# The thirty-third feature's Fourier weights: from own products to the sine product's free rows

## The chip, the core and the metric

The kernel runs on one core of one Trainium2 chip. A core has five engines that run at the same time, each through its own list of instructions and in the order of that list: TensorE (PE; its weight loads are shown as PEld), VectorE (DVE), ScalarE (ACT), GpSimd (POOL) and SyncE (SP), which here only issues transfers (its queue is shown as SPq). Products land in PSUM, a small memory of banks of 128 partitions x 512 f32; DVE and ACT read them from there ("evacuate" them) and so give the bank back to PE. Transfers between the chip's memory and SBUF, or within SBUF, run on 16 DMA engines. Engines wait for each other by semaphores only.

The metric is the device time of one execution in microseconds. It is measured in several runs. A further execution is profiled; the profile's span goes from its first instruction to its last.

## The reference, cut to what matters

Two inputs, a prompt of 256 positions and a sample of 2048, go through one encoder layer each, with the same weights. All is f32.

```python
F_GROUPS = 8; F_GROUP_DIM = 64; F_WIDTH = 512

def fourier_mix(u, w_f, b_f):
    b, s, _ = u.shape
    ug = u.astype(jnp.float32).reshape(b, s, F_GROUPS, F_GROUP_DIM)
    spec = jnp.fft.fft2(ug, axes=(1, 3), norm='ortho')
    mixed = spec.real.reshape(b, s, F_WIDTH).astype(u.dtype)
    return mixed @ w_f + b_f

def encoder_layer(x, ...):
    h = rms_norm(x, g_pre)
    q, k, v, z_a, u_f, z_f = jnp.split(h @ w_in, ...)
    y_a = neighbourhood_attention(q, k, v, rpb)
    y_f = fourier_mix(u_f, w_fourier, b_fourier)
    mixed = concatenate([rms_norm(y_a, g_na) * silu(z_a), rms_norm(y_f, g_f) * silu(z_f)])
    return x + rms_norm(mixed @ w_out, g_post)
```

The change lies in fourier_mix: a two-dimensional transform, over the positions and over the 64 features of each of eight groups, of which the real part is kept, and a product with the weights `w_fourier` (512 x 512).

## The kernel before, in words

**Stages.** The kernel computes the projections (q, k, v, z_a, z_f and u) for the sample first, with the transform over the positions half done; then comes the Fourier stage, 549 to 607 us, which the change touches; then the attention over 36 groups, and the output product. An f32 product with full precision is three passes here: both operands are split into a rounded "high" part (ACT copies it into the type fp32r) and a rest ("low", DVE subtracts), and `mm3` (L164 to L166) does high x high, high x low, low x high. So most products are followed by an ACT copy and a DVE subtraction: `split_ps` (L1016, L1017).

**The mathematics of the stage.** The real part of the transform over a group's 64 features is a cosine product minus a sine product. Feature s and feature 64 - s have the same cosines and opposite sines, so they are folded: 32 slots, s = 0 to 31, do for each of the two, plus the thirty-third, s = 32, whose cosine at frequency f is (-1)^f and whose sine is zero. Instead of transforming the data over the features, the kernel transforms the weights: `pq(0)` multiplies `w_fourier` with the cosines, `pq(1)` with the sines. The slot 0 of the sines is free, since sin 0 = 0: the table `cs` holds zeros there. The thirty-third feature's weights, `w32` (96 partitions x 512: eight groups at every fourth partition of three blocks of 32, the middle block for the low part), are made by products of their own in `pq32`, from a table `c32` of (-1)^f.

**Order of the stage on PE**, written by hand in the code: four groups `gq` 0 to 3, each of five column chunks c in `stage2` (tile `pab`; L1024 are the small products of `dft`, four of them for each chunk). Group 0 also makes `pny`, group 2 also the prompt's part `pup` (from `up` and `f256`). Results are split into AB (tiles `abh`, `abl`) and, for the chunk c = 4, into `a32`. Behind group 2 comes `pq(0)`, behind group 3 come `pq(1)` (L1062) and `pq32` (L1069). Then come the output products `y_mm` (tile `py`): for each block e of 128 output features (0 to 3) and each third ti of the columns, in the order 2, 0, 1, twelve products into p1 and p2 and one with `w32` and `a32`. `y_out` evacuates: ACT adds the bias (t1), DVE combines t1 and p2 into `Y` (L1276), a tile of 128 x 2304 f32 (1.2 MB) with two buffers. Y's prompt part is stored by L1302, the rest, 1 MB, by L1325, and `y0` is loaded from the stored prompt part (L1321) and from zD (L1322). ACT and POOL also make squares of Y for the norm.

**PSUM.** Eight banks: tag "a" has three (ppq, pny, pup, py1), "b" two (two thirds of the pab, and py2), "c" one (the other third of pab), "t" two.

**Buffers and transfers.** In this stretch the Tile scheduler orders the lists of ACT, DVE, POOL and SP; it does so ahead of time, and on the chip the order is fixed. All loads and stores here are issued by SP. In its order before: `f256` (L996), `up` (L998), the four loads of the last z tiles (L831), `cs` (L1001), `c32` (L1003, 192 KB), `wf` (L1005, 1 MB, the weights); then for the attention: the keys' rows `kl` (L1091, two halves), the tables `tb` (L1105, L1106, L1109), the queries `ql` (L1135), `v` (L1152, L1154), `za` (L1159), the output weights `wo` (L1234, eight loads), and the stores and loads of Y. A transfer takes one of eight completion semaphores in turn, and its issue waits until the transfer that is eight ahead in the list has landed; it also waits until its tile is free, or its data are there.

Of the kernel before, what the change touches and what calls it, by code (L numbers as in the profile page):

```python
# [10 lines left out]
F32 = mybir.dt.float32  # L11
F32R = mybir.dt.float32r
AF = mybir.ActivationFunctionType
ALU = mybir.AluOpType
# [29 lines left out]
def constants():  # L44
    c = {}
    c["ident"] = np.eye(128, dtype=np.float32)
    n1 = np.arange(128)
    f1 = np.zeros((128, 128))
    for k1 in range(64):
        f1[:, 2 * k1] = np.cos(2 * np.pi * ((k1 * n1) % 128) / 128)  # L50
        f1[:, 2 * k1 + 1] = np.sin(2 * np.pi * ((k1 * n1) % 128) / 128) if k1 else (-1.0) ** n1
    c["f1"] = f1.reshape(32, 4, 128).transpose(1, 0, 2).reshape(128, 128)
    nrm = 1.0 / np.sqrt(2048 * 64)
    n2 = np.arange(16)
    d = np.zeros((128, 16, 128))
    for g in range(16):
        for kl in range(4):
            k1 = 4 * g + kl
            for k2 in range(16):
                if k1:  # L60
                    k = k1 + 128 * k2
                elif k2 < 8:
                    k = 128 * k2
                else:
                    k = 64 + 128 * (k2 - 8)
                co = np.cos(2 * np.pi * ((n2 * k) % 2048) / 2048) * nrm
                si = np.sin(2 * np.pi * ((n2 * k) % 2048) / 2048) * nrm
                ca = k2 * 4 + kl
                cb = 64 + ca
                r0 = (kl * 2) * 16 + n2  # L70
                r1 = (kl * 2 + 1) * 16 + n2
                if k1:
                    d[r0, g, ca] = co
                    d[r1, g, ca] = -si
                    d[r0, g, cb] = si
                    d[r1, g, cb] = co
                else:
                    r = r0 if k2 < 8 else r1
                    d[r, g, ca] = co
                    d[r, g, cb] = si  # L80
    c["d2"] = d
    dn = np.zeros((128, 2))
    dn[:16, 0] = ((-1.0) ** n2) * nrm
    c["dnyq"] = dn
    n = np.arange(256)[:, None]
    k = np.arange(129)[None, :]
    ang = 2 * np.pi * ((n * k) % 256) / 256
    f256 = np.concatenate([np.cos(ang), np.sin(ang)], axis=1) / np.sqrt(256 * 64)
    c["f256"] = f256.reshape(4, 2, 32, 258).transpose(0, 2, 1, 3).reshape(128, 2, 258)
    f = np.arange(64)  # L90
    sl = np.arange(32)
    cs = np.zeros((128, 2, 64))
    c32 = np.zeros((128, 4, 96))
    for b in range(2):
        rows, cols = slice(64 * b, 64 * b + 64), slice(32 * b, 32 * b + 32)
        ang = 2 * np.pi * ((f[:, None] * sl[None, :]) % 64) / 64
        cs[rows, 0, cols] = np.cos(ang)
        cs[rows, 1, cols] = np.where(sl == 0, 0.0, np.sin(ang))
        for x in range(4):
            for r in range(3):  # L100
                c32[rows, x, 32 * r + 4 * (2 * x + b)] = (-1.0) ** f
    c["cs"] = cs
    c["c32"] = c32
    cm = np.zeros((128, 2, 40))
    cs_ = np.zeros((128, 80))
    rm = np.zeros((128, 48))
    for p in range(128):
        for b in range(2):
            ws = min(max(32 * b + p % 32 - 8, 0), 48)
            kc = 24 * b + np.arange(40)  # L110
            cm[p, b] = np.where((kc >= ws) & (kc < ws + 16), 0.0, BIG)
        i, qc = divmod(p, 16)
        for cb, j in ((0, slice(0, 24)), (1, slice(24, 56)), (3, slice(56, 80))):
            ws = min(max(16 * cb + qc - 8, 0), 48)
            kc = KC0[cb] + np.arange(KW[cb])
            cs_[p, j] = np.where((kc >= ws) & (kc < ws + 16), 0.0, BIG)
        for r0, j in ((max(i - 4, 0), np.arange(11)), (i, 11 + np.arange(15)), (min(i, 4), 26 + np.arange(12))):
            rm[p, j] = np.where((j - j[0] >= r0) & (j - j[0] < r0 + 8), 0.0, BIG)
    c["cmask"] = cm.reshape(128, 80)
    c["csmask"] = cs_  # L120
    c["rmask"] = rm
    return {k: np.ascontiguousarray(v.astype(np.float32)) for k, v in c.items()}
# [40 lines left out]
def mm3(nc, out, lh, ll, rh, rl, first, last):  # L163
    nc.tensor.matmul(out, lh, rh, start=first, stop=False)  # L164
    nc.tensor.matmul(out, lh, rl, start=False, stop=False)  # L165
    nc.tensor.matmul(out, ll, rh, start=False, stop=last)  # L166


def build(tc, A, O):
    nc = tc.nc  # L170
    es = ExitStack()
    es.enter_context(tc.manual_schedule(engines={mybir.EngineType.PE}))
    cst = es.enter_context(tc.tile_pool(name="cst", bufs=1))
# [28 lines left out]
    invt = cst.tile([128, 18], F32, name="invt")  # L202
    invf = cst.tile([128, 18], F32, name="invf")
    inva = cst.tile([128, 18], F32, name="inva")
    dnyq = cst.tile([128, 2], F32, name="dnyq")
    cm = cst.tile([128, 2, 40], F32, name="cm")


# [5 lines left out]
    ps = es.enter_context(tc.tile_pool(name="ps", bufs=3, space=PSUM))  # L214
    mmc = [0]

    def mmt(n):
        x = mmc[0] % 5 > 2
        mmc[0] += 1
        return ps.tile([128, n], F32, tag="t" if x else "a", name="mm", bufs=2 if x else 3)  # L220
# [10 lines left out]
    def gt(shape, dtype, name):  # L231
        return gp.tile(shape, dtype, tag="g", name=name)
# [152 lines left out]
    nq = {}  # L385
# [332 lines left out]
    for c in range(3, 6):  # L718
# [7 lines left out]
        if c == 4:  # L726
# [33 lines left out]
    for b in range(16):  # L760
# [13 lines left out]
        if 2 <= b < 8:  # L774
            x, y = divmod(b, 2)
# [7 lines left out]
        p = mmt(512)[:, :TP]  # L783
# [55 lines left out]
    for i in range(16):  # L839
# [48 lines left out]
        for j in range(7):  # L888
# [29 lines left out]
            if sg == 0:  # L918
                x, y = divmod(7 * (pr - 1) + j, 14)
# [17 lines left out]
            for f, d in ((u_load, 0), (u_split, 4), (u_stage1, 6)):  # L937
                x = 7 * pr + j - 7 - d
# [11 lines left out]
            p = mmt(512)  # L950
# [41 lines left out]
        nc.vector.memset(x, 0.0)  # L992
    pg = ExitStack()
    sm = pg.enter_context(tc.tile_pool(name="smF", bufs=1))
    f256 = sm.tile([128, 2, 258], F32, name="f256")
    nc.sync.dma_start(f256, A["f256"])  # L996
    up = sm.tile([128, 2, 512], F32, name="up")
    nc.sync.dma_start(up, uD.rearrange("(t p) c -> p t c", p=128))  # L998
    zgs.append(load_z(3))
    cs2 = sm.tile([128, 2, 64], F32, name="cs2")  # L1000
    nc.sync.dma_start(cs2, A["cs"])  # L1001
    c32 = sm.tile([128, 4, 96], F32, name="c32")
    nc.sync.dma_start(c32, A["c32"])  # L1003
    wf = sm.tile([128, 4, 512], F32, name="wf")
    nc.sync.dma_start(wf, A["wf"])  # L1005

# [8 lines left out]
    def split_ps(dh, dl, src, vec=False):  # L1015
        nc.vector.tensor_copy(dh, src) if vec else nc.scalar.copy(dh, src)  # L1016
        nc.vector.tensor_tensor(out=dl, in0=src, in1=dh.bitcast(F32), op=ALU.subtract)  # L1017
# [32 lines left out]
            dft(p, c, [(up[:, t], f256[:, t, 129 * m:129 * m + 129]) for t in range(2)])  # L1050
            split_ab(gq, c, lambda a: a[:, 1025:1154], p)

    PQ = []
    w32 = ab.tile([96, 512], F32R, name="w32")

    def pq(m):
        h = gt([128, 2, 512], F32R, "pqh")
        l = gt([128, 2, 512], F32R, "pql")
        for c in range(2):
            p = ps.tile([128, 512], F32, tag="a", name="ppq")  # L1060
            for x in range(2):
                nc.tensor.matmul(p[64 * x:64 * x + 64], cs2[:, m, :], wf[:, 2 * c + x, :], start=True, stop=True)  # L1062
            split_ps(h[:, c], l[:, c], p)
        PQ.append((h, l))

    def pq32():
        p = ps.tile([96, 512], F32, tag="a", name="ppq")
        for c in range(4):
            nc.tensor.matmul(p, c32[:, c], wf[:, c], start=c == 0, stop=c == 3)  # L1069
        nc.scalar.copy(w32, p)  # L1070
        nc.vector.tensor_tensor(out=w32[32:64], in0=p[32:64], in1=w32[32:64].bitcast(F32), op=ALU.subtract)

    for gq in range(4):
        for c in range(5):
            stage2(gq, zgs[gq], c)
        if gq == 2:
            pq(0)
    pq(1)
    pq32()
    pg.close()  # L1080

    KQ = T // 4
# [158 lines left out]
    sm = pg.enter_context(tc.tile_pool(name="smY", bufs=2))  # L1241
# [10 lines left out]
    def y_mm(e, ti):  # L1252
# [5 lines left out]
        for m, p in ((0, p1), (1, p2)):  # L1258
            for c in range(2):
                mm3(nc, p[:, :n], PQ[m][0][:, c, es_], PQ[m][1][:, c, es_],  # L1260
                    AB[m][0][:, c, cs], AB[m][1][:, c, cs], c == 0, m == 1 and c == 1)
# [109 lines left out]
    sm = pt.enter_context(tc.tile_pool(name="smA", bufs=2))  # L1371
# [202 lines left out]
    for k in range(2, len(G) + 1):  # L1574
        pr, i = divmod(k, 9)
        g, f = G[k] if k < len(G) else None, G[k - 1] if k else None
# [19 lines left out]
        x = k // 2 + 1  # L1596
# [62 lines left out]
        if 32 <= k < 36:  # L1659
            x, d = k - 32, atiles[k - 32]  # L1660
# [122 lines left out]
```

## Time and profile before

| | us |
|---|---|
| runs, without a profile | 970.62, 971.44, 972.39 |
| their median | 971.44 |
| the profiled execution, its span | 968.7 |
| of it, PE busy | 958.9 |

The clock granted to TensorE was 0.998 of full speed over the span. The page lists for each engine how long it was busy. The chain of waits is found from the end: from the last instruction back to what released it, or to the one before it on its engine, and so on. Rows of a timeline read "start, duration, engine, line, operation, output tile <- input tiles, shape", with the idle time ahead of it and what ended that in brackets; "x8" is a run of eight instructions, and then the duration is that of the whole run. Rows of a list of waits read "engine, line <- who released it: total, count, largest". A transfer's landing isn't in the timeline of its queue, whose rows are issues: it is read from the instruction that waits for it.

### The profile page before, as it was taken

What the parts mean: (1) busy time and instruction counts of PE and PEld (TensorE: products, weight loads), DVE (VectorE), ACT (ScalarE), POOL (GpSimd) and SP (SyncE); (2) the same over time, 40 slices, a digit from 0 to 9 for tenths busy, and PEclk for the clock granted to TensorE, in tenths of its full rate; (3) what the DMA queues carried; (4) which work ended last, traced back from release to release, by engine and by line L of the source; (5) the groups of instructions that cost most, each with busy time, mean ns of one, the idle gap of its engine ahead of it and who ended that gap; (6) DMA issues with size and microseconds to landing.
All of it is one profiled execution on the core that took longest, in us unless ns stands there. A gap on an engine that the chain in (4) does not pass through costs nothing.

```text
span 968.7 us, 17031 instructions
## 1 busy us (share of the span) xinstructions
PE 958.9 (99%) x5769; PEld 801.0 (83%) x5769; DVE 709.5 (73%) x1306; ACT 497.5 (51%) x1078; POOL 430.2 (44%) x400
## 2 busy tenths in 40 slices
PE   9999999999999999999999999999999999999997
PEld 7889988888888888888888879887788888878886
DVE  6768987777986867787777446776665656649997
ACT  6836675433325533333344255677666776744443
POOL 3100003464752202756654033577677686624544
PEclk9999999999999999999999999999999999999999
DMA  9899696556849996599989898698887998979993
GB/s 327 312 373 357 234 366 240 194 189 252 318 163 377 352 410 239 211 371 320 322 303 339 301 328 300 210 281 273 258 240 234 286 327 270 296 244 331 330 346 129
DMA packets 146450, 279.89 MB, mean 289 GB/s; under 512 B 13162, under 2 KB 84284, under 8 KB 142972
## 3 DMA queue, kind: packets, MB, share of 16 engines
q1 hardware_dynamic: 145932, 278.41, 82.4%
q8 instruction: 46, 0.75, 0.3%
q10 hardware_dynamic: 432, 0.39, 0.1%
q14 instruction: 40, 0.33, 0.1%
HBM read 184.37 MB, written 101.72 MB: 295 GB/s over the span
## 4 chain that ended last, share of the span: by engine, by line
PE 96%; DVE 1%; ACT 1%; issue 1%; POOL 1%; DMA 0%; DVEq 0%; SPq 0%; POOLq 0%; ACTq 0%
PE po L1432 19%; PE mm L165 18%; PE mm L164 18%; PE mm L166 18%; PE pv L1521 5%; PE ptb L1505 5%; PE s L1181 4%; PE pab L1024 2%; PE py L164 1%; PE py L166 1%; PE py L165 1%; DMA gpre<-gpre 0%; PE ppq L1062 0%; PE pz L166 0%; PE pz L164 0%
## 5 line engine op out<-in xcount | busy, mean ns | idle before, releaser
L164 PE MATMUL mm<-xh,wa 128*128 128x512 f32 x448 | 174.4, 389 | 0.0
L165 PE MATMUL mm<-xl,wa 128*128 128x512 f32 x448 | 174.3, 389 | 0.0
L166 PE MATMUL mm<-xh,wa 128*128 128x512 f32 x448 | 174.3, 389 | 0.0
L536 POOL TENSOR_TENSOR ws<-wr 128x512 f32<-128x512 f32 x16 | 22.2, 1386 | 226.6 <-DMA wr<-wz 222.8
L1215 POOL TENSOR_SCALAR w<-w,m 128x480 f32<-128x480 f32 (+6 forms) x136 | 86.0, 644 | 46.3 <-DVE m L1212 35.9
L164 PEld LDWEIGHTS mm<-xh,wa 128*128 128x128 f32 x448 | 84.1, 188 | 17.6
L166 PEld LDWEIGHTS mm<-xh,wa 128*128 128x128 f32 x448 | 84.1, 188 | 17.5
L165 PEld LDWEIGHTS mm<-xl,wa 128*128 128x128 f32 x448 | 84.1, 188 | 17.4
L1432 PE MATMUL po<-wo,yh 128*128 128x512 f32 x272 | 90.4, 413 | 0.0
L551 DVE TENSOR_TENSOR wa<-wr,wa 128x512 fp32r<-128x512 f32 x60 | 68.5, 1149 | 27.1 <-ACT wa L550 26.8
L1208 ACT ACTIVATE w<-w,m 128x480 f32<-128x480 f32 (+6 forms) x136 | 79.3, 586 | 17.1 <-DVE m L1203 17.1
L1432 PE MATMUL po<-w,yh 128*128 128x512 f32 x280 | 86.7, 391 | 0.0
L1203 DVE CUSTOM_DVE_ANT_1 w<-s,tb 128x360 f32<-128x360 f32 (+5 forms) x124 | 62.4, 541 | 10.3 <-PE s L1181 9.8
L589 POOL TENSOR_TENSOR mt<-mt,rmask 128x880 f32<-128x880 f32 (+2 forms) x24 | 51.0, 2139 | 34.1 <-DVE mt L585 27.6
L165 PE MATMUL mm<-vl,xh 128*128 128x512 f32 x168 | 65.5, 390 | 0.2 <-DVE vl L482 0.2
L164 PE MATMUL mm<-vh,xh 128*128 128x512 f32 x168 | 65.4, 389 | 0.0
L166 PE MATMUL mm<-vh,xl 128*128 128x512 f32 x168 | 65.4, 389 | 0.0
L877 DVE TENSOR_TENSOR f<-u,mm 128x512 f32<-128x512 f32 x64 | 43.5, 680 | 28.0 <-PE mm L166 23.1
L1432 PEld LDWEIGHTS po<-w,yh 128*128 128x128 f32 x280 | 52.3, 188 | 10.9 <-issue 0.2
L1505 PE MATMUL ptb<-ident,w 128*120 128x128 f32 (+5 forms) x428 | 59.5, 276 | 1.0 <-ACT nsb L1481 0.9
L550 ACT CAST wa<-wr 128x512 fp32r<-128x512 f32 x60 | 36.4, 617 | 44.1 <-PE mm L166 23.2
L1521 PEld LDWEIGHTS pv<-pt,v 120*64 120x64 f32 (+6 forms) x896 | 48.2, 136 | 12.8 <-issue 9.6
(263 smaller groups left out, 2394.3 us busy)
## 6 DMA issues: line engine op xcount, KB each, us to landing
wr<-wz SPq DMA_DIRECT2D x48, 512.0 KB
vl<-sD SPq DMA_DIRECT2D x20, 512.0 KB
xm<-xm SPq DMA_DIRECT2D x9, 1024.0 KB
oD<-ofs SPq DMA_DIRECT2D x18, 512.0 KB
of<-oD SPq DMA_DIRECT2D x18, 512.0 KB
yr<-yD SPq DMA_DIRECT2D x34, 256.0 KB
zD<-f SPq DMA_DIRECT2D x16, 512.0 KB
woD<-wo SPq DMA_DIRECT2D x16, 512.0 KB
```

The costliest lines, as they stand in the source:

```text
L164: nc.tensor.matmul(out, lh, rh, start=first, stop=False)
L165: nc.tensor.matmul(out, lh, rl, start=False, stop=False)
L166: nc.tensor.matmul(out, ll, rh, start=False, stop=last)
L551: nc.vector.tensor_tensor(out=o[:, 1], in0=src, in1=o[:, 0].bitcast(F32), op=ALU.subtract)
L589: nc.gpsimd.tensor_tensor(out=o, in0=i, in1=rmask[:, m0:m0 + n].unsqueeze(2).to_broadcast([128, n, 80]), op=ALU.add)
L877: nc.vector.tensor_tensor(out=dst(f, b), in0=src(uu[u]), in1=src(p), op=op)
L1203: nc.vector.tensor_tensor_reduce(out=rows(g["w"][b][:, h, :n], w), in0=rows(g["s"][2 * b + h][:, :n], w), in1=tv, scale=1.0, scalar=3.0e38 ...
L1208: nc.scalar.activation(w, w, AF.Exp, bias=m[:, h:h + 1], scale=-1.0, accum_out=m[:, 2 + h:3 + h])
L1215: nc.gpsimd.tensor_scalar(w, w, m[:, 4 + h:5 + h], 1.0, ALU.mult, ALU.mult)
L1432: nc.tensor.matmul(p, (d["l"] if x == 2 else d["h"])[:, c], w(n, int(x == 1), c), start=j == 0, stop=j == 11)
L1505: nc.tensor.transpose(ptb[h][:nk, j * 128:j * 128 + 128], g["w"][b][:, h, c0:c0 + nk], ident)
L1521: nc.tensor.matmul(p[hs, b], g["v"][:nk, v, hs], g["pt"][b][:nk, h, j * 128:j * 128 + 128], start=j == 0, stop=j == len(ch) - 1)
```

## The change

The sine table gets (-1)^f in its free slot 0, so that `pq(1)` makes the thirty-third feature's weights along with the sines' (partitions 0, 32, 64 and 96 of its two result tiles), and `pq32` with its table `c32` goes. For this,

- `pq(1)` moves from behind group 3 to between groups 1 and 2, and the loads of `cs` and `wf` move ahead of those of `f256`, `up` and the last z tiles;
- in `pq(1)`, DVE copies each result tile to an SBUF tile `nq` (two buffers), and for each of the two tiles three transfers of 4 x 512 f32 (8 KB) bring the four rows to their places in `nw` (96 x 512, filled with zeros by POOL before). They are issued by SP;
- the split of the sine product masks the free slot away with a third column of `dnyq` (0 at each 32nd partition, else 1): ACT's copy has it as a scale, and DVE's subtraction becomes a scalar_tensor_tensor, product x mask - high;
- `w32` is made from `nw` as it was from the product before, a copy by ACT and a subtraction by DVE.

```diff
-    dn = np.zeros((128, 2))
+    dn = np.zeros((128, 3))
     dn[:16, 0] = ((-1.0) ** n2) * nrm
+    dn[:, 2] = np.arange(128) % 32 != 0
...
-    c32 = np.zeros((128, 4, 96))
...
-        cs[rows, 1, cols] = np.where(sl == 0, 0.0, np.sin(ang))
-        for x in range(4):
-            for r in range(3):
-                c32[rows, x, 32 * r + 4 * (2 * x + b)] = (-1.0) ** f
+        cs[rows, 1, cols] = np.where(sl == 0, (-1.0) ** f[:, None], np.sin(ang))
...
+    cs2 = sm.tile([128, 2, 64], F32, name="cs2")
+    nc.sync.dma_start(cs2, A["cs"])
+    wf = sm.tile([128, 4, 512], F32, name="wf")
+    nc.sync.dma_start(wf, A["wf"])
+    nw = sm.tile([96, 512], F32, name="nw")
+    nc.gpsimd.memset(nw, 0.0)
     f256 = sm.tile([128, 2, 258], F32, name="f256")
     nc.sync.dma_start(f256, A["f256"])
     up = sm.tile([128, 2, 512], F32, name="up")
     nc.sync.dma_start(up, uD.rearrange("(t p) c -> p t c", p=128))
     zgs.append(load_z(3))
-    cs2 = sm.tile([128, 2, 64], F32, name="cs2")
-    nc.sync.dma_start(cs2, A["cs"])
-    c32 = sm.tile([128, 4, 96], F32, name="c32")
-    nc.sync.dma_start(c32, A["c32"])
-    wf = sm.tile([128, 4, 512], F32, name="wf")
-    nc.sync.dma_start(wf, A["wf"])
...
     def pq(m):
...
-            split_ps(h[:, c], l[:, c], p)
-        PQ.append((h, l))
-
-    def pq32():
-        p = ps.tile([96, 512], F32, tag="a", name="ppq")
-        for c in range(4):
-            nc.tensor.matmul(p, c32[:, c], wf[:, c], start=c == 0, stop=c == 3)
-        nc.scalar.copy(w32, p)
-        nc.vector.tensor_tensor(out=w32[32:64], in0=p[32:64], in1=w32[32:64].bitcast(F32), op=ALU.subtract)
+            if m == 0:
+                split_ps(h[:, c], l[:, c], p)
+                continue
+            nq_ = sm.tile([128, 512], F32, name="nq", bufs=2)
+            nc.vector.tensor_copy(nq_, p)
+            for r in range(3):
+                nc.sync.dma_start(nw[32 * r + 16 * c:32 * r + 16 * c + 16:4], nq_[::32])
+            nc.scalar.activation(h[:, c], p, AF.Copy, scale=dnyq[:, 2:3])
+            nc.vector.scalar_tensor_tensor(out=l[:, c], in0=p, scalar=dnyq[:, 2:3], in1=h[:, c].bitcast(F32),
+                                           op0=ALU.mult, op1=ALU.subtract)
+        PQ[m] = h, l
+        if m:
+            nc.scalar.copy(w32, nw)
+            nc.vector.tensor_tensor(out=w32[32:64], in0=nw[32:64], in1=w32[32:64].bitcast(F32), op=ALU.subtract)
 
     for gq in range(4):
         for c in range(5):
             stage2(gq, zgs[gq], c)
-        if gq == 2:
-            pq(0)
-    pq(1)
-    pq32()
+        if gq in (1, 2):
+            pq(2 - gq)
     pg.close()
```

By the order in which the scheduler puts the changed kernel's instructions on their engines, SP issues the six `nw` transfers behind the last z tiles' loads and ahead of `kl`; from there on the order of its transfers is that of before. ACT has, behind `pq(0)`'s first copy, the copy of `nw` to `w32`, and the copies of `kl` among those of group 3.

More of the change, by code (lines that the diff above doesn't have):

```diff
@@ L97, in constants @@
         cs[rows, 0, cols] = np.cos(ang)
-        cs[rows, 1, cols] = np.where(sl == 0, 0.0, np.sin(ang))
-        for x in range(4):
-            for r in range(3):
-                c32[rows, x, 32 * r + 4 * (2 * x + b)] = (-1.0) ** f
+        cs[rows, 1, cols] = np.where(sl == 0, (-1.0) ** f[:, None], np.sin(ang))
     c["cs"] = cs
-    c["c32"] = c32
     cm = np.zeros((128, 2, 40))
@@ L204, in build @@
     inva = cst.tile([128, 18], F32, name="inva")
-    dnyq = cst.tile([128, 2], F32, name="dnyq")
+    dnyq = cst.tile([128, 3], F32, name="dnyq")
     cm = cst.tile([128, 2, 40], F32, name="cm")
@@ L1051, in stage2 @@
             split_ab(gq, c, lambda a: a[:, 1025:1154], p)
-    PQ = []
+    PQ = {}
     w32 = ab.tile([96, 512], F32R, name="w32")
```

## The prediction

> **What bounds the kernel now.** I read the page first, then the waits, then the stretch that the change touches: the Fourier stage, 549 to 607 us. From the page, busy time and the chain by engine; from the list of waits, all of PE's from 545 us to the end:
>
> ```profile
> PE 958.9 (99%) x5769; PEld 801.0 (83%) x5769; DVE 709.5 (73%) x1306; ACT 497.5 (51%) x1078; POOL 430.2 (44%) x400
> ...
> PE 96%; DVE 1%; ACT 1%; issue 1%; POOL 1%; DMA 0%; DVEq 0%; SPq 0%; POOLq 0%; ACTq 0%
> ...
> PE ptb L1505 <- ACT nsb L1481: 0.9, 1, 0.9
> ```
>
> PE is the chain, and none of its waits stands in the Fourier stage. So PE work that goes should come off the end, unless a wait takes its place. The chain of waits in order of time (start, duration) shows what goes:
>
> ```profile
> 565.47 1.87 PE ppq L1062 x8
> 567.34 4.37 PE pab L1024 x54
> 571.71 1.87 PE ppq L1062 x8
> 573.58 3.60 PE ppq L1069 x8
> 577.18 0.17 PE py L164
> ```
>
> The 3.60 us at L1069 is pq32, the part removed. But a PE that never waits may still be close to waiting. The timelines of DVE, SP's queue and PE hold such a place, in the third pass (e = 2) of the output products:
>
> ```profile
> 594.21 1.34 DVE L1276 TENSOR_TENSOR Y<-t,py 128x252 f32<-128x252 f32 x7 [2.00 <-DMA yD<-Y]
> ...
> 585.41 0.33 SPq L1325 DMA_DIRECT2D yD<-Y  x1
> ...
> 596.44 0.34 PE L164 MATMUL py<-abh,pqh 128*128 128x384 f32 x1
> ```
>
> DVE stands still until the 1 MB store of pass 0's Y, issued at 585.41, has landed at about 594.1: Y has two buffers, so pass 2 writes into the tile that this store reads. Its seven combinations end at 594.21 + 1.34 = 595.55. They free the second of the two "b" banks for the p2 product that PE starts at 596.44. PE misses a stall by 596.44 - 595.55 = 0.89 us, some 0.8 after a hand-over. That margin, not the 3.60, decides the case: **if PE comes 3.60 us sooner and the store does not, PE stops there.**
>
> **The change part by part.** *PE.* pq32's eight passes go: -3.60 at 573.58. The sine product pq(1), 1.87, moves from behind group 3 to ahead of group 2; groups 2 and 3 then run 1.87 later and the first output product 3.60 earlier. Between group 3 and the output products 1.87 + 3.60 = 5.47 us of PE work covered the evacuation; now nothing does.
>
> ```profile
> 560.29 0.84 PE pab L1024 x8
> ...
> 559.62 0.66 PE L1024 MATMUL pup<-f,up 128*128 128x129 f32 x4
> ...
> 565.40 1.94 PE L1062 MATMUL ppq<-wf,cs 128*64 128x512 f32 x8
> ...
> 566.52 0.59 ACT L1016 CAST pqh<-ppq 128x512 fp32r<-128x512 f32 x1 [0.74 <-PE ppq L1062]
> ...
> 551.06 0.40 DVE L1016 CAST abh<-pab 128x256 fp32r<-128x256 f32 x1
> ...
> 567.14 0.69 DVE L1017 TENSOR_TENSOR pql<-ppq,pqh 128x512 fp32r<-128x512 f32 x1 [1.03 <-ACT pqh L1016]
> ...
> 572.02 0.42 DVE L1017 TENSOR_TENSOR abl<-pab,abh 128x256 fp32r<-128x256 f32 x1 [0.99 <-ACT abh L1016]
> ...
> 572.85 0.42 DVE L1033 TENSOR_TENSOR a<-pab,a 32x256 fp32r<-32x256 f32 x1 [0.41 <-ACT a L1031]
> ...
> 577.83 0.68 DVE L1071 TENSOR_TENSOR w<-ppq,w 32x512 fp32r<-32x512 f32 x1 [2.90 <-ACT w L1070]
> ```
>
> Group 3 ended at 571.71; its last abl was done 0.73 later, its a-part 1.56 later. The products need the last abl only after nine matmuls of 0.17 (1.5) and the a-part after twelve (2.0). Covered, with 0.4 us to spare; uncovered it would cost up to the 0.6 of ACT's w32 copy, which now runs in that stretch.
>
> *DVE and ACT in group 2.* DVE gets two copies of 128x512 (by the 128x256 row some 0.67 each), the masked pql stays at 0.69 and ACT's pqh at 0.59. DVE worked 2.07 of 4 us there (the second row of the table below), so 1.34 more fits; a bank held longer can cost PE 0 to 0.7 us. I take 0, because what PE loses here it finds again at the Y wait. The zero fill of nw is POOL's, which is idle.
>
> *The queue.* Here something moves that the words of the change do not say: the six nw transfers stand in SP's order behind group 3's zg loads and ahead of the two kl loads, and with them of everything that follows. SP works in order.
>
> ```profile
> 551.55 0.38 SPq L996 DMA_DIRECT2D f<-f  x1
> 551.98 0.78 SPq L998 DMA_DIRECT2D up<-uD  x1
> ...
> 555.75 0.44 SPq L1005 DMA_DIRECT2D wf<-wf  x1
> 556.58 1.33 SPq L1091 DMA_DIRECT2D kl<-kD  x2
> ...
> 559.97 0.92 SPq L1152 DMA_DIRECT2D v<-vP  x2
> 562.79 0.34 SPq L1159 DMA_DIRECT2D za<-zD  x1
> 565.18 0.38 SPq L1135 DMA_DIRECT2D ql<-qD  x1
> ...
> 595.58 0.32 SPq L1302 DMA_DIRECT2D yD<-Y  x1
> ...
> 597.56 0.37 SPq L1321 DMA_DIRECT2D y<-yD  x1
> ```
>
> The waits of SP's own queue say what two of these issues waited for, and the windows (PE, PEld, DVE, ACT, POOL busy, clock, DMA share, GB/s) how full the transfer engines were:
>
> ```profile
> SPq L1135 <- DMA kl<-kD: 2.0, 1, 2.0
> ...
> SPq L1159 <- DMA wf<-wf: 1.9, 1, 1.9
> ...
> SPq L1321 <- DMA yD<-Y: 0.9, 1, 0.9
> ```
>
> ```profile
> 557.00:561.00 4.00, 4.00 (x55) 3.87 (x54) 2.13 (x6) 1.76 (x5) 0.00 (x0) 1.00 1.05 395
> 561.00:565.00 4.00, 4.00 (x60) 3.88 (x61) 2.07 (x6) 1.92 (x6) 0.00 (x0) 1.00 1.01 408
> ...
> 569.00:573.00 4.00, 4.00 (x51) 2.99 (x50) 1.66 (x5) 3.18 (x8) 2.01 (x3) 1.00 0.80 188
> 573.00:577.00 4.00, 4.00 (x13) 1.41 (x9) 1.66 (x3) 1.54 (x4) 4.00 (x4) 1.00 0.96 330
> 577.00:581.00 4.00, 4.00 (x24) 3.98 (x23) 1.56 (x7) 1.44 (x3) 1.26 (x2) 1.00 0.95 270
> 581.00:585.00 4.00, 4.00 (x25) 4.00 (x24) 2.45 (x9) 1.34 (x3) 0.00 (x0) 1.00 1.05 400
> 585.00:589.00 4.00, 4.00 (x25) 4.00 (x24) 1.98 (x13) 3.38 (x9) 0.00 (x0) 1.00 1.08 383
> ```
>
> *When kl can go.* Group 2 began at 559.62 - 0.95 = 558.7 (its first four pab products, eight passes of the row at 560.29 with a slow start); pq(1) now starts there. The product is ready 566.52 - 565.40 = 1.12 after PE's first pass. Then, since ACT is ordered behind the copy: copy 0.67, pqh 0.59, pql 0.69, second copy 0.67, with hand-overs 562.5. Three issues of 0.47 (two v loads took 0.92) follow: kl goes out at 563.9 instead of 556.58. Before, its early issue was worth little: the bytes queued behind wf, which landed at 562.79, and kl's first half landed at 565.18. Now it meets an empty queue. The small y store, 0.13 MB at some 400 GB/s, landed at most 1.98 after its issue (595.58 to 597.56), so 1.65 is the latency, and 0.59 MB at 400 GB/s take 1.5: kl lands at 567.0, **1.8 us later** than before. That is the lower bound of the delay at this point: 565.18 is the landing of the slowest of 16 engines. The upper bound goes by bytes: kl's began at 562.79 - 1.65 = 561.1 at the earliest and now begin by 564.5, **3.4**. c32's 0.2 MB, 0.5 us of moving, is gone, but it was moved ahead of this gap and gives nothing back.
>
> *Does the delay last?* From 573 to 589 the transfer engines are full, 0.95 to 1.08; only 569 to 573 is thin, 0.80, and could absorb 4 x 0.2 = 0.8. The order of all that follows (tb, v, za, wo, ql, the Y store) is as before, and each issue there waits for a landing before it. So the store lands later by s = 1.0 to 3.4; I take 2.8, because the rows around it are full and the thin stretch is made by v's small rows, which come along.
>
> [...]
>
> *The sum.* PE would reach that product at 596.44 - 3.60 = 592.84. DVE starts at 594.21 + 2.8 = 597.0, ends at 598.35, and PE goes on at about 598.45: 2.0 us later than before, in place of 3.60 earlier. In general the kernel changes by s - 0.8: +0.2 for s = 1.0, +2.6 for 3.4. Queued behind DVE's held combinations are the rest of pass 2's, ACT's square of Y and the store that feeds y0; they move with PE, and POOL's y0 product had 2.4 us of its own wait. Span 968.7 + 2.0 = 970.7; the runs' median 971.44 has 2.7 around the span, which I leave, so **973.4**.
>
> **The rivals.**
>
> *The whole gain* (not slower): -3.60, 967.8. It needs the store to land 2.8 us sooner than before. For it: 96% of the chain is PE, c32's load is gone. Against: the order of SP's queue and full transfer engines.
>
> *The queue catches up*, s of 0 to 1: -0.8 to +0.2, about 971.1. For it: the thin stretch at 569 to 573, 270 GB/s at 577 to 581, and that kl's lag was one engine's. Against: shares near 1 there all the same.
>
> *The six transfers are served one after another.* At 1.98 each, the time of the small y store, they need 11.9 us; kl's bytes come behind them at 572.4 instead of 563.9, s = 11.3, and the kernel ends 10.5 later, 982. If only two or three follow each other, +4 to +6. It decides as soon as nw's landings stand more than 1 us apart. Against: v's two loads left 0.47 apart while others were under way.
>
> [...]
>
> **How the numbers follow.** A measurement of this kernel tells about 0.2%, 1.9 us, from no change. Held by the store: 0.74, of it 0.48 above +1.9 (s above 2.7) and 0.26 within. Whole gain 0.12, catching up 0.07 (within), one after another 0.07 (slower). So faster 0.12, same 0.33, slower 0.55. The held case alone spans 971.6 to 974.1. The range, 970.0 to 976.0, adds the catching up (970.6) below and the milder case of transfers in series (+4, 975.4) above, and leaves out the whole gain and the rest of the serial case, under 0.2 together.
>
> **What would show it.** Right: L1069 gone; kl's issue at about 564 behind six nw issues; the Y store landing at 596 to 598; DVE's wait for yD<-Y at 5 to 7 us; a PE wait at py of 4 to 6 us where none was, the rest of the timeline moved by one constant. Wrong: no PE wait at py and a span near 965; kl landing by 566; or PE waiting before 580, for wf or nw, which would be another case altogether: wf takes the queue's place after cs, at 551.98 in place of 555.75, 3.8 sooner; by that it lands at 562.79 - 3.8 = 559.0, but it no longer stands behind zg(3)'s and up's bytes, so sooner, against a need at 558.7.

## The result, and the profile after

The changed kernel takes 979.2 us (median of six runs, 977.56 to 981.45); the kernel before, measured beside it, 971.38 (six runs, 970.62 to 973.35). The ratio is 1.0064 with a 95% interval of 1.0048 to 1.008. That is slower, by more than forecast: the medians stand 7.8 us apart, where 2.0 was said, and 979.2 lies above the range.

The profiled execution spans 979.7; it is the slowest of the six (their spans go from 975.8 to 979.7). The page shows the same busy time of PE (eight passes are gone, but some of the others are slower, as is seen below) and another chain:

```profile
PE 959.6 (98%) x5761; PEld 802.0 (82%) x5761; DVE 711.2 (73%) x1308; ACT 497.5 (51%) x1078; POOL 429.9 (44%) x401
...
PE 49%; DMA 3%; DVE 2%; ACT 1%; issue 1%; SPq 1%; POOL 1%; DVEq 0%; ACTq 0%; POOLq 0%
```

These shares add up to 58%; for the rest the page names nothing, so the chain is read in the stretch itself. PE's list of waits has one large new row:

```profile
PE py L160 <- DVE Y L1275: 8.7, 1, 8.7
```

It is the place that the prediction named. Before comparing times, one has to see where the two executions stand at the start of the Fourier stage. This is the first product of group 0 in the kernel before:

```profile
549.14 1.00 PE L1024 MATMUL pab<-d,zg 128*128 128x64 f32 x8
```

and the same in the changed kernel, with DVE's held combinations and PE's held product in pass 2 (idle time and what ended it in brackets):

```profile
551.52 1.00 PE L1020 MATMUL pab<-d,zg 128*128 128x64 f32 x8
...
602.79 2.34 DVE L1275 TENSOR_TENSOR Y<-t,py 128x252 f32<-128x252 f32 x10 [11.59 <-DMA yD<-Y]
...
604.28 0.66 PE L160 MATMUL py<-abh,pqh 128*128 128x384 f32 x1 [8.69 <-DVE Y L1275]
604.74 0.52 PE L161 MATMUL py<-abl,pqh 128*128 128x384 f32 x1
```

This execution enters the stage 551.52 - 549.14 = 2.4 us later than the one before. The change does not touch what runs there; the other executions of the study enter it between 0 and 2.3 us late (wo_behind_y, with the changed order of loads, 0.0; before_wo4, without it, 1.4), so it is the spread of the runs, and it is taken off below. With it taken off, the Y store of pass 0 lands 602.79 - 594.21 - 2.4 = 6.2 us later than before (said: 2.8), and PE passes the held product 604.28 - 596.44 - 2.4 = 5.4 later (said: 2.0). The rest comes behind it: PE's passes of 128x384, 0.34 us in the kernel before, take 0.52 here. The windows say why (PE, PEld, DVE, ACT, POOL busy, clock, DMA share, GB/s):

```profile
561.00:565.00 4.00, 4.00 (x36) 2.55 (x27) 2.82 (x6) 1.69 (x4) 0.00 (x0) 1.00 0.75 284
565.00:569.00 4.00, 4.00 (x56) 3.88 (x56) 2.99 (x9) 2.44 (x7) 0.00 (x0) 1.00 0.35 77
...
577.00:581.00 4.00, 4.00 (x25) 4.00 (x24) 1.53 (x9) 1.59 (x4) 4.00 (x4) 1.00 0.25 63
...
597.00:601.00 4.00, 0.00 (x0) 0.00 (x0) 0.00 (x0) 0.00 (x0) 0.48 (x1) 0.87 1.08 415
601.00:605.00 4.00, 0.72 (x2) 0.75 (x3) 2.21 (x10) 0.42 (x1) 0.28 (x1) 0.50 0.55 229
605.00:609.00 4.00, 4.00 (x14) 4.00 (x14) 1.41 (x8) 0.17 (x1) 0.45 (x1) 0.50 0.62 183
```

While PE stood, the granted clock fell to half (0.50 in the last two windows), and it stayed there until about 610 (by the trace's clock record from 599.94 to 610.18). The seventeen passes from the held product on cost 2.6 us more than before; the pass that started at 599.42 before starts at 609.87 here, 10.45 - 2.4 = 8.1 us later.

The windows also show two holes in the transfers, where the kernel before had none: 0.35 in 565 to 569 and 0.25 in 577 to 581. SP's queue shows what it was doing meanwhile (start, duration of a run of issues):

```profile
562.95 3.64 SPq L1065 DMA_DIRECT2D nw<-nq  x6
566.64 1.05 SPq L1090 DMA_DIRECT2D kl<-kD  x2
569.26 1.82 SPq L1151 DMA_DIRECT2D v<-vP  x2
...
573.60 1.06 SPq L1151 DMA_DIRECT2D v<-vD  x2
577.17 2.03 SPq L1153 DMA_DIRECT2D v<-vD  x1
579.25 0.74 SPq L1158 DMA_DIRECT2D za<-zD  x1
...
593.78 0.33 SPq L1324 DMA_DIRECT2D yD<-Y  x1
```

Its waits give two landings:

```profile
SPq L1153 <- DMA tb<-tD: 2.5, 1, 2.5
SPq L1151 <- DMA kl<-kD: 1.3, 1, 1.3
```

The wait for kl is that of the v load at 573.60: it took the semaphore of kl's second half. The wait for `tb` is not new: the kernel before has it too, at its v load of 570.11:

```profile
SPq L1154 <- DMA tb<-tD: 2.4, 1, 2.4
```

The first hole lies between the last z tile and kl, whose issue waited behind the six transfers. The second lies around the v load at 577.17.

### The profile page after: what moved, and what is told of

Same layout as the page of the kernel before. It is cut to its first block, busy times and chain, and to the rows that moved or that the text cites. A ratio compares the mean times of both kernels' runs of the same rounds, so it can differ in the third digit from the quotient of the medians.

```text
span 979.7 us, 17029 instructions
## 1 busy us (share of the span) xinstructions
PE 959.6 (98%) x5761; PEld 802.0 (82%) x5761; DVE 711.2 (73%) x1308; ACT 497.5 (51%) x1078; POOL 429.9 (44%) x401
## 4 chain that ended last, share of the span: by engine, by line
PE 49%; DMA 3%; DVE 2%; ACT 1%; issue 1%; SPq 1%; POOL 1%; DVEq 0%; ACTq 0%; POOLq 0%
PE po L1431 19%; PE pv L1520 5%; PE ptb L1504 5%; PE s L1180 4%; PE mm L162 3%; PE mm L161 3%; PE mm L160 3%; PE pab L1020 2%; DMA wo<-woD 1%; DMA yD<-Y 1%; DMA wr<-wz 1%; PE py L160 1%; PE py L161 1%; PE py L162 1%; DMA tD<-mt 0%
## 5 line engine op out<-in xcount | busy, mean ns | idle before, releaser
L547 DVE TENSOR_TENSOR wa<-wr,wa 128x512 fp32r<-128x512 f32 x60 | 70.6, 1184 | 27.4 <-ACT wa L546 27.1
```

The lines of the kernel that those rows point to most:

```text
L547: nc.vector.tensor_tensor(out=o[:, 1], in0=src, in1=o[:, 0].bitcast(F32), op=ALU.subtract)
```

## The experiments

Each kernel was compared with the kernel before on the same chip. Times are medians, ratios come with their 95% interval.

| run | us | before, beside it | ratio | PE's largest wait, 545 to 625 us |
|---|---|---|---|---|
| the change | 979.2 | 971.4 | 1.0064 (1.0048 to 1.008) | py 8.7 |
| no_transfers | 979.0 | 971.5 | 1.0075 (1.0059 to 1.009) | pab 2.3 |
| nw_by_pool | 974.4 | 971.5 | 1.0022 (1.0006 to 1.0038) | pab 1.7 |
| keep_pq32 | 976.8 | 971.5 | 1.0054 (1.0035 to 1.0073) | py 3.4 |
| wo_behind_y | 978.2 | 971.5 | 1.0068 (1.0051 to 1.0085) | first output product 6.6 |
| ordered_direct | 971.9 | 971.9 | 0.9993 (0.9978 to 1.0008) | py 1.1 |
| ordered_pool | 972.9 | 971.9 | 1.001 (0.9995 to 1.0026) | py 2.8 |
| ordered_pool_wo4 | 972.6 | 971.9 | 1.0002 (0.9988 to 1.0017) | ptb 1.0 |
| before_wo4 | 974.5 | 971.9 | 1.0029 (1.0016 to 1.0043) | ptb 1.0 |
| kl_ahead | 975.4 | 971.9 | 1.0035 (1.0023 to 1.0047) | py 4.6 |
| pool_wo2 | 971.6 | 971.9 | 0.9993 (0.9984 to 1.0001) | ptb 1.0 |
| pool_wo4_y0 | 971.3 | 971.9 | 0.999 (0.9978 to 1.0003) | ptb 1.0 |
| filled_wait | 977.0 | 972.9 | 1.0046 (1.0029 to 1.0064) | none |

**no_transfers: take the six transfers away.**

```diff
-            for r in range(3):
-                nc.sync.dma_start(nw[32 * r + 16 * c:32 * r + 16 * c + 16:4], nq_[::32])
```

> The changed kernel without its six nw transfers; w32 is made from the zero fill, so the thirty-third feature's share is left out of the result. All else of the change stays: early cs and wf, pq(1) between groups 1 and 2, DVE's copies, the mask, no pq32. Queue theory (the six transfers stand ahead of kl in SP's order, the transfer engines run dry, and pass 0's Y store lands late): SP can issue kl right behind the z tiles at about 557, the store lands near 594, PE's wait at py shrinks from 8.7 us to between 0 and 3, and the time is 967.5 to 971. Rival on PSUM (DVE's two copies and the masked split hold the banks of tag a longer and groups 2 and 3 lose the time): the loss stays, 977 to 980. Rival on the loads (cs and wf ahead of the z tiles are what makes the queue late): the wait at py stays above 6 us, 977 to 980.

kl went out at 558.61 (this execution entered the stage 2.3 late) and there was no wait at py, as the queue theory has it, and yet the time was that of the changed kernel. The run was spoilt by its own edit. With nothing but a zero fill to wait for, w32's copy on ACT and its subtraction on DVE were put ahead of group 0's evacuations, and PE stopped there:

```profile
557.15 1.94 PE L1020 MATMUL pab<-d,zg 128*128 128x64 f32 x8 [2.34 <-DVE abl L1013]
```

The windows of this kernel show what followed:

```profile
553.00:557.00 4.00, 1.81 (x17) 1.72 (x16) 2.02 (x7) 2.28 (x3) 0.00 (x0) 0.88 0.73 212
557.00:561.00 4.00, 3.85 (x43) 3.85 (x43) 2.26 (x13) 0.91 (x4) 0.00 (x0) 0.50 0.98 391
...
569.00:573.00 4.00, 4.00 (x13) 1.42 (x9) 2.17 (x4) 0.69 (x1) 0.00 (x0) 0.50 0.93 239
573.00:577.00 4.00, 4.00 (x37) 4.00 (x36) 2.45 (x7) 2.35 (x7) 0.00 (x0) 0.98 0.77 238
```

The clock was at half from 557 to 573 (0.50 in each of the four windows), though PE was busy for 3.85 to 4.00 of each 4 us. The rival on PSUM expected 977 to 980 and is not borne out by the hit: the wait is in group 0, ahead of the changed pq(1). As a test of the transfers the run says nothing; as a first sight of the clock it says much.

**nw_by_pool: issue the six transfers from GpSimd.**

```diff
-                nc.sync.dma_start(nw[32 * r + 16 * c:32 * r + 16 * c + 16:4], nq_[::32])
+                nc.gpsimd.dma_start(nw[32 * r + 16 * c:32 * r + 16 * c + 16:4], nq_[::32])
```

> The changed kernel with the six nw transfers issued by GpSimd, which is idle there, in place of SP; nothing left out. Queue theory: kl is no longer behind them, so the same 967.5 to 971 as without the transfers, provided that they land before the first use of w32 at about 577; a wait at py of 0 to 3 us. If it is not their place in SP's order but their own slowness (rows brought one after another, w32 late), PE waits at its product with w32 and the time stays above 974. Rivals on PSUM and on the early loads: 977 to 980.

kl went out at 556.44, pass 0's store at 585.65 (585.41 before), and the wait at py was gone: moving six issues to another queue undoes most of the loss. The median did not reach 971. The new order had put ACT's copies of kl and of nw among the evacuations of groups 2 and 3. The copies of kl waited for nothing there, but that of nw stood 1.8 us for its landing, with the copies of pq(0) behind it, and PE waited in group 3:

```profile
PE pab L1020 <- DVE abl L1013: 1.7, 1, 1.7
```

The clock behind it was 0.78 and 0.79 in the windows from 573 to 581; these are means of 4 us, which half speed from 575.2 to 578.7 gives. The profiled execution took 971.25, one of the two fastest of ten (971.21 to 978.81): the wait and the slow clock ate PE's lead there, and what the slower executions lost besides is not shown.

**keep_pq32: give PE its 3.60 us back.**

```diff
-            nc.scalar.copy(w32, nw)
-            nc.vector.tensor_tensor(out=w32[32:64], in0=nw[32:64], in1=w32[32:64].bitcast(F32), op=ALU.subtract)
...
         if gq in (1, 2):
             pq(2 - gq)
+    pq32()
```

> The changed kernel with pq32 and its table kept behind group 3, w32 made from it as before, while the six transfers still run and fill nw, which nothing reads. PE has its 3.60 us of work back. Queue theory: PE stops at the same landing of the store, so its wait at py falls from 8.7 by about 3.6 to 5 us and the time stays within 2 of the changed kernel, 977 to 981. If the time of the changed kernel were set by PE's own work or by PSUM, it would be 3.6 longer, 982 to 984. If the wait only exists because PE comes 3.6 us too early, it goes, and the time is 971 to 974.

```profile
PE py L165 <- DVE Y L1287: 3.4, 1, 3.4
```

The removed work was put back and the kernel became no slower: 976.8 against 979.2. The wait is shorter by 5.3, not by 3.6, because the store was also less late in this run (by the trace's record of its semaphore 598.87, which is 4.2 behind the kernel before where the changed kernel has 6.2); the time is a little below the band. Not 982: what ends the stage is the store. Not 974: the wait does not come from PE's being early alone.

**wo_behind_y: bring the store forward.** The eight wo loads go behind the stores of passes 0 and 1:

```diff
-    for n in range(2):
-        for c in range(4):
-            nc.sync.dma_start(wo1[n][c].bitcast(F32),
-                              woD[1, :, c, :, n * 512:n * 512 + 512].rearrange("x p d -> p x d"))
...
             nc.sync.dma_start(yD[1, e, :, TP:], Y[:, TP:])
+            if e < 2:
+                for c in range(4):
+                    nc.sync.dma_start(wo1[e][c].bitcast(F32),
+                                      woD[1, :, c, :, e * 512:e * 512 + 512].rearrange("x p d -> p x d"))
```

> The changed kernel with the eight wo loads (4 MB) issued behind the Y stores of passes 0 and 1 in place of ahead of them; nw still ahead of kl. Queue theory: 4 MB at some 400 GB/s are 10 us, so pass 0's store lands some 8 us sooner, PE never waits at py, and the time is that of before less 3.6 plus at most 1 for group 2: 967.5 to 969.5, unless wo is then late for the first output product at about 620. Rivals on PSUM and group 2: no change, 977 to 980.

The store went out at 581.98, there was no wait at py, and PE was 3.1 us ahead of the kernel before up to the first output product. The time did not follow, because the next load was then late: y0's, which now stood behind wo. From the waits of PE and of DVE:

```profile
PE po L1431 <- ACT y0h L1349: 6.6, 1, 6.6
...
DVE y L1347 <- DMA y<-zD: 5.8, 1, 5.8
```

Behind this wait the clock was at half, 0.50 in the window from 609 to 613. The expectation had allowed for wo itself being late, not for y0.

**ordered_direct, ordered_pool, ordered_pool_wo4, before_wo4.** Four runs without the accident on ACT. A constraint holds ACT's copies of kl behind pq(0)'s first copy, where they were before the change, and w32's behind group 3's last (ACL lists ACT's copies in their order, PQI is the place of that first copy):

```diff
+    with tc.issue_after(ACL[-1].ins):
+        nc.scalar.copy(w32, nw)
...
+    with tc.issue_after(ACL[PQI].ins):
+        for x in range(4):
+            split_k(KK[0], x)
```

The first has no transfers and makes w32 from `nq`, so it leaves out the thirty-third feature's share; the second has them on GpSimd; the third also moves four wo loads behind pass 0's store; the fourth moves these four in the kernel before.

> The changed kernel without the six transfers; w32 is made from the first 96 partitions of the second nq tile, so it holds wrong rows and the thirty-third feature's share is left out. In place of the scheduler's order ACT's copies of kl are held behind pq(0)'s first copy, as before the change, and w32's copy behind group 3's last. Store theory: kl goes out near 557 and pass 0's Y store lands near 594 as before; PE comes 3.1 to 3.6 us sooner, so it waits 2 to 3 us at py in pass 2 and the gain is 0.5 to 0.8: 970.5 to 971.2, up to 972.5 if that wait also lowers the granted clock. If the store does not hold PE: 967.5 to 968.3. If DVE's copies and the masked split cost PE in groups 2 and 3: a wait at pab there of 1 us or more, and 972 or more.

> The changed kernel, complete, with the six transfers issued by GpSimd and the same two orders on ACT as in the run above (kl's copies behind pq(0)'s first, w32's behind group 3's last). If the 1.7 us wait at pab and the lower clock of the run with GpSimd's transfers came from ACT standing at w32's and kl's copies, both go: no wait at pab, PE 3.1 to 3.6 us sooner at pass 2, a wait at py of 2 to 3 us for the store, 970.5 to 972.5. If the transfers by GpSimd are late themselves, the wait moves to the first product with w32 and the time stays at 973 or more.

> The run above with four of the eight wo loads (2 MB) issued behind pass 0's Y store. At some 400 GB/s they are 5 us, so the store lands at about 589 and no longer holds PE. Store theory: no wait at py, the full gain of 3.1 to 3.6 us: 967.8 to 968.6. If another wait stands right behind (the loads for y0, as with all eight moved): a wait at the first output product, 970 or more.

> The kernel before with the same four wo loads behind pass 0's Y store and nothing else. Store theory: the store lands 5 us sooner too, but PE had no wait there, so nothing is gained: 971.0 to 971.9. If moving the loads is worth something by itself (the transfer engines less crowded later): 968 to 970.

Neither of the first two has a wait at pab any more, so DVE's two copies and the masked split cost PE nothing that shows. PE, some 3 us ahead, waits for the store. In ordered_pool, PE's waits and DVE's row are

```profile
PE py L160 <- DVE Y L1279: 2.8, 1, 2.8
PE py L1266 <- DVE w L1081: 0.6, 1, 0.6
...
596.15 2.33 DVE L1279 TENSOR_TENSOR Y<-t,py 128x252 f32<-128x252 f32 x10 [5.69 <-DMA yD<-Y]
```

The 2.8 is what was expected; the 0.6 is for w32, which the constraint puts late. ordered_direct waited 1.1 at py, less than the 2 to 3 expected: its execution came into the stage 2.3 late, with the store not late by as much (DVE started at 596.04, 1.8 behind the kernel before). Both kernels stand where the kernel before stands, within their intervals. So without the gap, the 3.60 us of PE work saved are worth nothing that these runs can tell (ordered_direct's interval would allow 2.1 us): the store takes most of them. Nor do the times tell ordered_pool from nw_by_pool; that the accident on ACT is gone shows in the waits alone.

The other two missed what the store theory said of them. In ordered_pool_wo4 the wait at py is gone and the time is still 972.6, as its second branch had it; before_wo4 is slower by 1.0029, though the same move should have been free there. What the two share is behind 600 us. The chain of waits of before_wo4:

```profile
595.95 5.92 DMA yD<-Y
...
601.94 4.51 DMA y<-yD
```

Pass 2's prompt part goes out at 595.95 and takes 5.92 us to land, y0's load then 4.51. In the profile of before, both together were over sooner: y0's load had gone out at 597.56, here at 601.94, of which 1.4 is this execution's late entry. Bytes moved out of the store's way are in the way of y0.

**kl_ahead: change the dose.** Transfers on SP as in the change, but kl's two loads ahead of them (ACT's copies of kl held as above, w32's behind pq(0)'s second copy): the lines move from behind the stage to ahead of its loop.

```diff
+    sc = load_k(0)
+    KK = {0: load_k(0)}
+    for x in range(2):
+        fetch_k(KK[0], 0, x)
     for gq in range(4):
         for c in range(5):
             stage2(gq, zgs[gq], c)
```

> The changed kernel, complete, its six transfers on SP as in the change, but the two kl loads issued ahead of them; ACT's copies of kl and of nw held as in the ordered runs. Only the dose changes: behind the transfers stands all that follows but not kl's 1.15 MB, which keep the engines busy for 2.9 us more at some 400 GB/s. Queue theory: the store lands some 3 us sooner than in the changed kernel, the wait at py falls from 8.7 to 5 or 6 us, and the time is 975 to 977.5. If the late kl alone were the cause (its copies on ACT, say), moving it ahead would give 970.5 to 973.

```profile
PE py L160 <- DVE Y L1280: 4.6, 1, 4.6
```

975.4, inside the band of the queue theory: with 1.15 MB less behind the six transfers the wait falls from 8.7 to 4.6, and it does not go. So what stands behind the waiting issues counts. By how much is less sure: the store lands 3.0 behind the kernel before here, against 6.2 in the changed kernel's profile, but against 4.2 and 4.0 in keep_pq32 and filled_wait, which have the changed kernel's queue.

**pool_wo2, pool_wo4_y0: a version that beats both?** Transfers by GpSimd, w32's copy earlier, two or four of the wo loads behind pass 0's store, y0's load (`y0l`) ahead of pass 2's store. With two loads:

```diff
     for n in range(2):
-        for c in range(4):
+        for c in range(4 - 2 * n):
...
+            if e == 2:
+                with tc.issue_after(y0l.ins):
+                    nc.sync.dma_start(yD[1, e, :, TP:], Y[:, TP:])
...
+            if e == 0:
+                for c in range(2, 4):
+                    nc.sync.dma_start(wo1[1][c].bitcast(F32),
+                                      woD[1, :, c, :, 512:1024].rearrange("x p d -> p x d"))
```

> The changed kernel, complete, transfers by GpSimd, kl's copies on ACT as before the change, w32's copy behind pq(0)'s second (so the 0.6 us wait for w32 goes), two of the eight wo loads (1 MB, 2.5 us) behind pass 0's Y store, and y0's load ahead of pass 2's Y store. Store theory: of the wait of 2.8 at py at most 0.5 is left, PE keeps 2.5 to 3.6 us, 968 to 969.8, which is faster than both kernels. If the two loads are then missed further on, as in the runs with four: 971 to 973 with a wait at the first output product or at ptb.

> The same with four wo loads behind pass 0's Y store. No wait at py; what the kernel before lost with these four loads moved (2.6) came behind 606 us, at the first output product and at ptb. If that came from y0's load standing behind pass 2's Y store, it goes here: 968 to 969.5. If it came from wo itself: 971 to 973.

Both are faster than the changed kernel; neither can be told from the kernel before (0.9993 and 0.999, both intervals reach 1), so both came out by their second branch. PE has no wait at py and no wait for w32, and, with each execution's late entry taken off, 3.1 to 3.3 us of lead up to about 606. Half of the lead goes at the start of the attention, ahead of the transposes (`ptb`), in two waits of 1.0 and 0.5; more goes later, and at the end of the two profiles 0.8 and 0.6 are left. All four runs with two or four wo loads behind pass 0's store have these two waits at ptb, with y0's load ahead of pass 2's store or not. The chain of pool_wo2 says through what:

```profile
593.84 5.35 DMA yD<-Y
...
599.24 2.76 DMA y<-yD
...
602.13 1.03 POOL y L1327
...
603.18 0.63 ACT y0h L1361
...
603.83 0.69 DVE y0h L1363
...
608.10 1.28 DVE Y L1279 x6
```

Once more a small store, 0.13 MB, lands 5.35 us after its issue among a crowd of large transfers (their share is 0.91 in the window from 593 to 597), and the first attention tiles hang on it.

**filled_wait: keep PE busy in the wait.**

```diff
+        if e == 2 and ti == 1:
+            for _ in range(40):
+                nc.tensor.matmul(p1[:, :n], PQ[0][0][:, 0, es_], AB[0][0][:, 0, cs], start=True, stop=True)
```

> The changed kernel with 40 more products (128 x 384, 0.17 us each, 6.9 us in all) on PE just ahead of the output product that waits; their sums are overwritten. PE arrives 6.9 us later at a wait of 8.7, so some 1.8 is left of it. If the 2.6 us that the products behind the wait took longer come from a clock that falls while PE stands idle, they go, and the kernel with 6.9 us more of PE work is the faster of the two: 976 to 977.3 where the changed kernel took 979.2. If the clock has nothing to do with the idle time, the time stays: 978.5 to 980. If the wait were not for a fixed landing, the work would add up: 982 or more.

```profile
593.80 7.10 PE L1259 MATMUL py<-abh,pqh 128*128 128x384 f32 x40
600.75 0.33 PE L160 MATMUL py<-abh,pqh 128*128 128x384 f32 x1
...
601.97 0.34 PE L160 MATMUL py<-abh,pqh 128*128 128x384 f32 x1
```

Forty useless products, and the kernel is not slower but, by the medians, 2.2 us faster than the changed one, by the ratios 1.8 (the two intervals overlap, so the profile decides). No wait was left where 1.8 was expected, since the store landed sooner than in the changed kernel's profile; DVE's row shows it:

```profile
600.15 2.34 DVE L1278 TENSOR_TENSOR Y<-t,py 128x252 f32<-128x252 f32 x10 [9.36 <-DMA yD<-Y]
```

The product that waited is the one at 601.97: it takes 0.34, not 0.66, and the passes behind it 0.34, not 0.52. The clock was 1.00 in the windows from 589 to 609. The 2.6 us behind the wait were the clock's.

## Why the prediction was wrong

**Right: the place and the mechanism.** pq32's time did not come off the end; pass 0's Y store, late through SP's order, held DVE and DVE held PE. keep_pq32 (no gain from PE's work alone), kl_ahead (the dose) and ordered_pool (the transfers off SP's queue) show it. Of the signs, kl's issue came at 566.64 - 2.4 = 564.2 (said: 564), DVE's wait for the store at 11.59 (said: 5 to 7) and PE's at 8.69 (said: 4 to 6). The relation of the sum, the kernel changes by s - 0.8, holds up to the held product: s = 6.2 gives 5.4, and 5.4 was measured there; kl_ahead's s = 3.0 gives 2.2, measured 2.2.

**Wrong: the size of s**, in the step "Does the delay last?". At kl's first half the delay was as bounded: by the trace's record of the semaphores this half landed at 570.57, in the kernel before at 565.17, which is 3.0 later with the 2.4 taken off; the bounds were 1.8 and 3.4. From there I let the delay only shrink, since the engines were full behind it. It grew instead. With the 2.4 off, the v load of L1153 went out 4.7 late, and the za load behind it 6.3 late. In the kernel before these two were

```profile
570.11 0.41 SPq L1154 DMA_DIRECT2D v<-vD  x1
570.56 0.49 SPq L1159 DMA_DIRECT2D za<-zD  x1
```

Of the growth of 3.3, 1.6 is the v issue itself, 2.03 us long in place of 0.41. The other 1.7 came in between the two halves of kl: the v load that waits for the second half started at 573.60 here and at 566.63 before, already 4.6 late, and the halves landed 3.0 apart here, 1.4 before. The wait for `tb` behind them added nothing (2.5 here, 2.4 before). Three other kernels with the same queue (keep_pq32, wo_behind_y, filled_wait) have kl's halves 1.4 apart and the long v issue; in keep_pq32 and filled_wait the store was 4.2 and 4.0 late. So the 1.7 is in this one profile of the four, that of the slowest of six executions, and its cause stays open; the growth at the v issue is in all four, and in keep_pq32 and filled_wait it is enough to take s above 3.4. Behind that issue the next large load, `tb`, goes out late, and the engines run dry a second time (0.25). What lengthens the v issue stays open: it took 2.17, 2.03, 1.73 and 2.09 in the other four kernels with the transfers on SP's queue, 0.25 to 0.56 in those that had them on GpSimd, 0.25 in ordered_direct and before_wo4, but 1.71 in no_transfers.

**Missing: the clock.** The sum let PE go on at full speed after a wait that it put at 5.6 us itself. No wait of that length stands in the profile of before, so its rows could not show the price: 2.6 us on the seventeen passes behind 8.7 us of wait, 1.6 on as many behind 3.4 (keep_pq32), nothing in filled_wait, where PE did not stand. Among products of 128x384 the clock did not fall with a wait of 2.8 us (ordered_pool, 1.00 in its windows up to 605); it fell with waits of 3.4 (keep_pq32; the window of 601 to 605 has 0.58, its mean), 4.6 (kl_ahead; 0.50 in 597 to 601) and 8.7 (the change). Among small products it fell with shorter ones: 1.7 (nw_by_pool) and 2.3 (no_transfers).

**Smaller steps.** PE fell idle ahead of the held product at 604.28 - 8.69 = 595.59, which with the 2.4 off is 3.2 ahead of 596.44, not 3.6; the pass at 596.44 in the kernel before starts 0.17 before the one ahead of it ends (596.27, 0.34 long), so the lead was some 3.4. Group 2 cost nothing, as taken: its start moved by 562.93 - 558.7 - 2.4 = 1.8, which is pq(1). That the six transfers go one after another, the rival at 982, is refuted: they left SP 0.6 apart and landed 0.5 to 0.9 apart (564.70 to 567.73 by the record of their semaphores), not 2. That the profiled execution, 981.45, stands near the 982 of that rival is chance. "The queue catches up" did not happen in any run with the transfers on SP.

So 2.0 was made of 3.60 saved and 5.6 waited; what came was 5.4 at the held product and 2.6 of clock, some 8 in the profiled execution and 4.7 to 7.8 by the ratio's interval. With the 4.0 to 4.2 that the store was late in the two kernels beside it, the same sum gives 3.2 to 3.4; with the clock that is, as an estimate, some 6.

## What to carry to other kernels

An instruction that waits in a queue can cost not its own time but that of the bytes behind it: with 1.15 MB less behind the six transfers the wait at py fell from 8.7 to 4.6 us (kl_ahead). So ask which queue can take it where nothing stands behind, before asking whether PE gets faster. A delay bounded at its first landing was not bounded further on, where each issue waits for an earlier landing: 3.0 us at kl's first half, 6.2 at the store. And price a new PE wait twice: for its length, and for the slow clock behind it, which here cost 2.6 us behind 8.7 and 1.6 behind 3.4 among the products of 128x384, and came with 1.7 and 2.3 among small ones. Where PE and the transfers are both nearly full, as here, work taken from PE alone is worth little until the next landing also comes earlier: pq32's 3.60 us less left 971.9 against 971.9 (ordered_direct).

## What the runs showed of the hardware that was not expected

- In stretches of small products a shorter wait brought the clock down, and it stayed down while PE was busy: 2.34 us in no_transfers (products of 128x64), then 0.50 in the windows from 557 to 573; 1.7 us in nw_by_pool, then 0.78 and 0.79 in those from 573 to 581. Waits of 1.0 us at ptb brought none (1.00 in all windows around them in ordered_pool_wo4, before_wo4, pool_wo2 and pool_wo4_y0). Behind the 8.7 us of the changed kernel, among products of 128x384, full speed was back at 610.18, after 5.9 us of work. That the size of the products makes the difference is not shown: no run changed it alone.
- The clock was at half for 10.24 us in the change, by its trace's clock record. By the windows (for each, 4 us x 2 x (1 - its mean)) it was for 3.4 in keep_pq32 and in nw_by_pool, 6.9 in kl_ahead and 17.1 in no_transfers. What sets these lengths is not shown.
- One issue on SP's queue took 2.03 us in the change where the same transfer's took 0.41 in the kernel before.
- A store of 0.13 MB, pass 2's, landed 5.35 (pool_wo2) and 5.92 us (before_wo4) after its issue where large transfers were under way: their share was 0.91 in 593 to 597 in the one, 1.03 in 597 to 601 in the other. In the profile of before that same store landed within 1.98 (0.77 in 593 to 597), and those of passes 0 and 1, issued behind the wo loads, 7.8 and 6.6 after theirs (by the record of their semaphores).
